# Weighted transposes with TensorE sums for the last tokens, early eviction of the fifth down product, and new PSUM bank use, in a one-core diffusion transformer layer

## The chip, the cores and the metric

The kernel runs on one core of a Trainium2 chip. The metric is device microseconds for one execution. The engines are named as in the profile: PE is TensorE's matmul, PEld its weight load, DVE VectorE, ACT ScalarE, POOL GpSimd, SP SyncE, which here issues DMAs.

## The reference

One layer over 1024 latent tokens of width 1024 with 256 context tokens, in float32: modulation by a conditioning vector, windowed and global grouped-query attention in parallel, a gated merge and an output projection, a residual LayerNorm, a feed-forward block with a depthwise convolution of width 3, and a second residual LayerNorm. Only the part from the first LayerNorm on matters here:

```python
def _conv_ffn(h, w_up, conv_w, conv_b, w_down):
    u = h @ w_up
    u = lax.conv_general_dilated(u, conv_w[:, None, :], ...) + conv_b
    gate, val = jnp.split(u, 2, axis=-1)
    return (jax.nn.silu(gate) * val) @ w_down
...
x = _layer_norm(DEEPNORM_ALPHA * x + gate1 * y, ln1_g[l], ln1_b[l])
h = x * (1.0 + scale2) + shift2
y = _conv_ffn(h, w_up[l], conv_w[l], conv_b[l], w_down[l])
x = _layer_norm(DEEPNORM_ALPHA * x + gate2 * y, ln2_g[l], ln2_b[l])
```

`w_up` has 2 x 2816 columns, `w_down` 2816 rows. `_layer_norm` subtracts the mean over the 1024 channels, scales by rsqrt(var + 1e-5), and applies a gain and a bias per channel.

## The kernel before, in words

**Products.** Activations lie with channels on the partitions and tokens along the free axis: eight channel tiles `f` of 128, two halves of 512 tokens. Every float32 product is three matmuls in a reduced type, `mm3` (L90 to L92): high x high, low x high and high x low. The high part is a ScalarE cast (L82), the low part a subtraction on VectorE or POOL (L87); both are made by `split` from raw tiles that DMAs bring.

**LN1 and the up projection.** LN1 runs in three token slices of 512, 256 and 256. For each slice `ln_steps` gives a list of steps: `stats` (TensorE column sums against a column of ones, L1028 and L1029, then tiny VectorE steps and a `pow` on POOL for the reciprocal root), `diags` (two diagonal tiles, L976), `cast` (two products with a tile of ones that spread the reciprocal root and the mean over all partitions, L1044, each copied from its PSUM bank to SBUF by ScalarE, L1046), and one `apply` for each channel tile (a multiplication L1051, a subtraction L1053, then the output). The steps wait in a list `pend`; `tick` counts TensorE's work in nanoseconds as it is written down, and lets a step into the program when its delay has gone by. For LN2 these delays are the tuples `LN2_D` (tokens 0 to 511, slice "b0") and `LN2_E` (512 to 767, "b1"): before the statistics, the diagonals, the broadcast, the first `apply`, and each further one.

The first three of 22 column blocks of the up projection are plain (`up_conv`): products on banks `u`, then the convolution `conv3` from these banks, one ScalarE pass (L1237) and two VectorE passes (L1238, L1240). The other blocks use seven products of half size with sums of weights and of the tiles `B`; those sums, `T13` and `T24`, are built by `build` (`t` on VectorE and POOL, L1075; high parts by ScalarE, L1113; low parts L1075) while the plain blocks run.

**The down projection.** It is seven products again, in the order 1, 6, 2, 7, 4, 5, 3, each over eleven inputs `k`. A product of `product(p)` fills four PSUM banks for 512 tokens, and two sets of four banks alternate (`sides`). For each input a DMA brings `rd`, ScalarE makes `hd`, VectorE `ld`. A finished product is added to the residual `zz` out of PSUM by VectorE (`accum`, L1418) in callbacks of the list `evict`, which the next product works off. LN2's slice b0 is ready when the fourth of product 4's results has been evicted, inside product 5; its steps then run by `LN2_D` in product 5: all eight multiplications on VectorE, all eight subtractions on POOL, the eight output passes `of` on ScalarE (`emit2`, L1411). Product 3 follows in two token slices of 256 with outputs `yl` (`last_mm`). Its high and low parts for inputs 0 to 6 are made long before (`D3AT`), those for 7 to 10 behind product 5's. In slice b1 the old order runs over the four `f`, inside each over inputs 0 to 6, and then again over the four `f` with inputs 7 to 10. Then the accumulations, the square sums, and the steps of LN2 by `LN2_E` follow.

**The last 256 tokens** are transposed (`tok`, L1541) so that tokens lie on partitions: two tiles of 128 tokens, each in two PSUM banks `zt`. VectorE takes the statistics from there (`bn_stats`, L1544, `bn_aggr`), POOL the `pow`, ScalarE writes `ot` = (z - mean) x rstd (L1597), and VectorE and POOL multiply by the gain and add the bias as rows `lnr` (L1586, L1588); four DMAs send the result out.

**What sets the order.** TensorE's order is the order of the program text. The other engines' queues are ordered by a scheduler from its own estimates; each engine then takes its queue strictly in turn. The functions stand below, with the line numbers of the profile.

## Time and profile before

| | us |
|---|---|
| median of 3 runs | 1600.74 (1598.96, 1600.74, 1603.09) |
| the profiled execution | 1601.19 |
| its span, first to last instruction | 1599.1 |
| TensorE busy | 1531.7 |
| VectorE, ScalarE, POOL busy | 1198.4, 813.2, 747.9 |
| mean granted TensorE clock | 0.989 |

Times of the profile count from the span's start. A row of the timeline is start, length, engine, line, operation, output<-inputs without the numbers of buffers, and in brackets how long the engine had been idle and what ended that. A matmul's length overlaps the next one's; the distance of the starts is what it costs. In the windows, each engine has its busy time and, in brackets, its instructions.

### The profile page before, as it was taken

Reading aid. Unit: us, or ns where it says so; the run is one execution under the profiler, and the core shown is the slowest. Engines: PE = TensorE matmul, PEld = TensorE weight load, DVE = VectorE, ACT = ScalarE, POOL = GpSimd, SP = SyncE. Lnnn points to the kernel's source line nnn. Section 1 sums busy time; section 2 is a strip of 40 time slices with the busy share of each in tenths; the row PEclk is TensorE's granted clock in tenths of the full one; section 3 lists DMA queues with packets and bytes.
Section 4 is the critical chain, followed back from the end, with each engine's and each line's share of the span. In section 5 each row is a group of like instructions: output and inputs, shape, how many; then the busy total and the mean of one; then the engine's idle time right before and its main releaser. Section 6 shows DMA issues by size and latency. Waiting matters only on the chain.

```text
span 1599.1 us, 22063 instructions
## 1 busy us (share of the span) xinstructions
PE 1531.7 (96%) x7680; PEld 1271.6 (80%) x7680; DVE 1198.4 (75%) x1766; ACT 813.2 (51%) x1443; POOL 747.9 (47%) x731
## 2 busy tenths in 40 slices
PE   6999999999999999999999988999999999999996
PEld 5878788888877887777688977888888888888876
DVE  7797646638888777788674887688888888657886
ACT  5422222458887566688431664454444444435542
POOL 0573302526666556565332563466767665021142
PEclk9999999999999999999999998999999999999998
DMA  9695662322237555540550222333334446996721
GB/s 377 217 317 182 217 214 80 119 81 67 58 113 161 128 138 127 124 86 18 177 179 19 93 67 92 106 106 105 106 106 109 116 119 176 375 263 209 253 100 53
DMA packets 112367, 229.98 MB, mean 144 GB/s; under 512 B 12960, under 2 KB 27808, under 8 KB 112160
## 3 DMA queue, kind: packets, MB, share of 16 engines
q1 hardware_dynamic: 96816, 198.93, 37.2%
q0 software_dynamic: 10400, 20.19, 8.2%
q10 hardware_dynamic: 5040, 9.46, 1.6%
q8 instruction: 60, 0.98, 0.3%
q14 instruction: 51, 0.42, 0.1%
HBM read 177.35 MB, written 65.86 MB: 152 GB/s over the span
## 4 chain that ended last, share of the span: by engine, by line
PE 75%; DVE 10%; ACT 4%; issue 4%; POOL 3%; DMA 3%; ACTq 0%; SPq 0%; DVEq 0%; POOLq 0%
PE ptr L531 5%; PE p L90 4%; PE p L92 4%; PE p L91 4%; PE b L92 3%; PE b L91 3%; PE b L90 3%; PE g L90 2%; PE g L92 2%; PE g L91 2%; PE av L552 2%; PE s L414 2%; PE d L91 2%; PE c L91 2%; PE a L91 2%
## 5 line engine op out<-in xcount | busy, mean ns | idle before, releaser
L541 DVE TENSOR_TENSOR ptl<-ptr,pth 128x512 fp32r<-128x512 f32 x188 | 124.7, 685 | 27.4 <-ACT pth L540 25.2
L531 PE MATMUL ptr<-ident,p 128*128 128x128 f32 x816 | 126.5, 278 | 10.4 <-DVE ptl L541 8.1
L540 ACT CAST pth<-ptr 128x512 fp32r<-128x512 f32 x188 | 106.5, 588 | 56.4 <-PE ptr L531 32.6
L87 DVE TENSOR_TENSOR ld<-rd,hd 128x1024 fp32r<-128x1024 f32 x77 | 94.0, 1240 | 53.3 <-ACT hd L82 51.0
L426 ACT ACTIVATE p<-p,nm 128x1024 f32<-128x1024 f32 (+2 forms) x128 | 125.4, 981 | 11.2 <-DVE p L459 10.5
L531 PEld LDWEIGHTS ptr<-ident,p 128*128 128x128 f32 x816 | 93.7, 140 | 40.3 <-DVE ptl L541 13.8
L82 ACT CAST hd<-rd 128x1024 fp32r<-128x1024 f32 x77 | 79.2, 1050 | 81.5 <-PE p L92 55.2
L552 PE MATMUL av<-pth,VT 128*128 128x512 f32 x236 | 104.7, 444 | 1.0 <-ACT avs L558 0.5
L90 PE MATMUL p<-hd 128*128 128x512 f32 x264 | 103.2, 391 | 0.0
L92 PE MATMUL p<-hd,ld 128*128 128x512 f32 x264 | 102.7, 389 | 0.0
L91 PE MATMUL p<-ld,hd 128*128 128x512 f32 x264 | 102.7, 389 | 0.0
L90 PE MATMUL g<-hh,whg 128*128 128x512 f32 x256 | 99.9, 390 | 0.0
L92 PE MATMUL g<-hh,wlg 128*128 128x512 f32 x256 | 99.7, 389 | 0.0
L553 PE MATMUL av<-ptl,VT 128*128 128x512 f32 x236 | 97.7, 414 | 2.0 <-POOL ptl L87 1.9
L91 PE MATMUL g<-hl,whg 128*128 128x512 f32 x256 | 99.6, 389 | 0.0
L87 POOL TENSOR_TENSOR wlg<-wg,whg 128x512 fp32r<-128x512 f32 x32 | 45.0, 1415 | 109.6 <-ACT whg L82 107.3
L459 DVE TENSOR_SCALAR_CACHE_REDUCE p<-s,cvt,nmc 128x1024 f32<-128x1024 f32 x64 | 84.5, 1340 | 12.2 <-PE s L415 12.0
L414 PE MATMUL s<-KL,q 128*128 128x512 f32 (+2 forms) x192 | 76.0, 396 | 2.9 <-ACT p_x L426 2.0
L82 ACT CAST wA<-ru 128x512 fp32r<-128x512 f32 x57 | 35.5, 623 | 76.6 <-PE d L92 34.1
L188 DVE CUSTOM_DVE_ANT_0 wml<-wml,sc,bmc 128x1024 f32<-128x1024 f32 x32 | 44.4, 1397 | 40.0 <-DMA wml<-in_wmodT_dram 37.9
L84 POOL TENSOR_SCALAR pth<-prw 128x512 fp32r<-128x512 f32 x48 | 31.1, 647 | 89.0 <-ACT prw L537 63.1
L415 PE MATMUL s<-KL,q 128*128 128x512 f32 (+2 forms) x192 | 71.6, 373 | 0.0
(396 smaller groups left out, 4989.3 us busy)
## 6 DMA issues: line engine op xcount, KB each, us to landing
wml<-in_wmodT_dram SPq DMA_DIRECT2D x48, 512.0 KB
ru<-in_w_up_dram SPq DMA_DIRECT2D x38, 512.0 KB
rd<-td SPq DMA_DIRECT2D x55, 256.0 KB
rd<-sd SPq DMA_DIRECT2D x44, 256.0 KB
rd<-in_w_dn_dram SPq DMA_DIRECT2D x33, 256.0 KB
wm<-in_wmodT_dram SPq DMA_DIRECT2D x16, 512.0 KB
wg<-in_w_g_dram SPq DMA_DIRECT2D x32, 256.0 KB
sgd<-sg ACTq DMA_DIRECT2D x32, 256.0 KB
```

Source lines behind the costliest of these rows:

```text
L82: nc.scalar.copy(hi, src)
L87: lo_eng.tensor_tensor(out=lo, in0=src, in1=hi.bitcast(F32), op=ALU.subtract)
L90: nc.tensor.matmul(ps, a[0], b[0], start=start, stop=False, skip_group_check=resumed)
L91: nc.tensor.matmul(ps, a[0], b[1], start=False, stop=False, skip_group_check=resumed)
L92: nc.tensor.matmul(ps, a[1], b[0], start=False, stop=stop, skip_group_check=resumed)
L414: nc.tensor.matmul(o, self.q[0][:, hs], ks, start=True, stop=False)
L426: nc.scalar.activation(p, s, AF.Exp, bias=nm[:, h:h + 1], scale=scale, accum_out=sm[:, h:h + 1])
L531: nc.tensor.transpose(tr[:, h * P:(h + 1) * P], self.pslice(h, n), ident)
L540: nc.scalar.copy(hi, tr)
L541: nc.vector.tensor_tensor(out=lo, in0=tr, in1=hi.bitcast(F32), op=ALU.subtract)
L552: nc.tensor.matmul(self.av, v, hi, start=first, stop=False)
L553: nc.tensor.matmul(self.av, v, lo, start=False, stop=self.left == 0)
```

## The change

- `cast` puts the two broadcast products of a slice of 256 tokens into the two halves of one PSUM bank (LN1's second and third slice, LN2's b1).
- Product 5 is added to the residual in eight `accum` calls right behind the product, ahead of the loads of product 3's last inputs, and the square sums come behind. The banks of what follows are given by hand (`pst`): slice b1's `yl` on one set of four, the transposes of channels 4 to 7 and the last slice's `yl` on the other, those of channels 0 to 3 on b1's.
- Product 3's slice b1 has the input outermost: for each of the eleven inputs all four `f`.
- For the last 256 tokens ScalarE writes the square and z x gain (`prep`); TensorE transposes the weighted tile, and sums z and its square per token by matmuls with a column of ones into a bank `st`, zeroed by a product first. The statistics come from `st`; `lnr[0]` is negated, and the end is one VectorE pass from PSUM (mean x negated gain + transposed) and one (x rstd + bias) for each of the four output tiles; one of the latter is done by ScalarE and POOL.
- The delays of LN2 are new numbers.

```diff
-LN2_D = 5000.0, 4000.0, 2500.0, 1500.0, 700.0
-LN2_E = 3500.0, 3000.0, 1500.0, 800.0, 500.0
+LN2_D = 2500.0, 500.0, 3500.0, 500.0, 700.0
+LN2_E = 5500.0, 500.0, 3500.0, 500.0, 500.0
-OTP = (0, 0), (1, 0)
+OTP = (0, 0),
...
         def cast():
+            both = sml(f"bc{nm}") if 2 * w <= HALF else None
             for i, a in enumerate("rm"):
-                ps = sml(f"bc{a}{nm}")[:, 0:w]
+                ps = sml(f"bc{a}{nm}")[:, 0:w] if both is None else both[:, i * w:(i + 1) * w]
                 nc.tensor.matmul(ps, onesf, bcs[i], start=True, stop=True)
...
-            else:
-                accum(f + 4, h1, o, False)
-                sums(f + 4, LN2_S[1], f == 0)
-
-        evict += [lambda f=f, o=acc[f]: ev(f, o) for f in range(4)]
+        if p != 5:
+            evict += [lambda f=f, o=acc[f]: ev(f, o) for f in range(4)]
         if p == 4:
             after.append(lambda: pend.extend(ln_steps(zs2, zq2, h0, "b0", emit2, *LN2_D, LN2_P[0])))
-    banks[:] = sides[nside[0] % 2] + sides[nside[0] % 2 ^ 1]
+    yb, ab = sides[nside[0] % 2], sides[nside[0] % 2 ^ 1]
+    banks[:] = [yb[3]]
+    for f in range(4):
+        accum(f + 4, h1, acc[f], False)
+        accum(f, h1, acc[f], True)
     d3 += [dload(3, k, ring) for k in range(len(D3AT), NH)]
-    for e in evict:
-        e()
+    hfree += xs
     for f in range(4):
-        accum(f, h1, acc[f], True)
+        sums(f + 4, LN2_S[1], f == 0)
 
     s = LN2_S[-1]
     w = s.stop - s.start
     nt = w // P
-    zt = {}
-    bst = post.tile([P, nt, 2, 6], F32, tag="bst", name="bst")
-    mv = post.tile([P, nt, 2], F32, tag="bmv", name="bmv")
-    nm = post.tile([P, nt], F32, tag="bnm", name="bnm")
+    def pst(n, name):
+        return ps4.tile([P, HALF], F32, tag=f"r{n}", name=name)
+    pr = [ht(f"pr{n}", (P, 4, w)) for n in range(4)]
+    nc.vector.tensor_scalar(out=pr[0][:, 3, 0:P], in0=ident, scalar1=ln2c[:, 3:4], scalar2=None, op0=ALU.mult)
+    nc.gpsimd.tensor_scalar(out=lnr[0], in0=lnr[0], scalar1=-1.0, scalar2=0.0, op0=ALU.mult, op1=ALU.add)
+    zt = {1: [pst(n, f"zt1_{n}") for n in ab[0:2]]}
+    zero4 = post.tile([P, 8], F32, tag="zero4", name="zero4")
+    nc.vector.memset(zero4, 0.0)
+    def prep(f):
+        nc.scalar.activation(pr[2 + f // 4][:, f % 4], zv(f, s), AF.Square)
+        if f != 3:
+            nc.scalar.activation(pr[f // 4][:, f % 4], zv(f, s), AF.Identity, scale=ln2c[:, f:f + 1])
 
     def tok(f):
-        if f % 4 == 0:
-            zt[f // 4] = [sml(f"zt{f}_{t}", keep=True) for t in range(nt)]
+        z, g = zv(f, s), pr[f // 4][:, f % 4]
+        if f == 4:
+            nc.tensor.matmul(st[:, 0:2 * nt], ident, zero4[:, 0:2 * nt], start=True, stop=True)
         for t in range(nt):
-            nc.tensor.transpose(zt[f // 4][t][:, (f % 4) * P:(f % 4 + 1) * P],
-                                zv(f, slice(s.start + t * P, s.start + (t + 1) * P)), ident)
-            if f % 4 == 3:
-                nc.vector.bn_stats(out=bst[:, t, f // 4], in_=zt[f // 4][t])
-
-    todo = [4, 5, 6, 7]
+            ts = slice(t * P, (t + 1) * P)
+            nc.tensor.matmul(st[:, t:t + 1], z[:, ts], onec, start=False, stop=True, skip_group_check=True)
+        for t in range(nt):
+            ts = slice(t * P, (t + 1) * P)
+            o = zt[f // 4][t][:, (f % 4) * P:(f % 4 + 1) * P]
+            if f == 3:
+                nc.tensor.matmul(o, z[:, ts], pr[0][:, 3, 0:P], start=True, stop=True)
+            else:
+                nc.tensor.transpose(o, g[:, ts], ident)
+        for t in range(nt):
+            ts = slice(t * P, (t + 1) * P)
+            nc.tensor.matmul(st[:, nt + t:nt + t + 1], pr[2 + f // 4][:, f % 4, ts], onec, start=False, stop=True,
+                             skip_group_check=True)
 
     def last_mm(o, f, r, ks):
         q = slice(r.start - HALF, r.stop - HALF)
@@ -1554,51 +1573,51 @@
             tick((r.stop - r.start) / 0.8)
 
     r = LN2_S[1]
-    yl = [sml(f"yl{f}")[:, 0:r.stop - r.start] for f in range(4)]
+    yl = [pst(n, f"yl{f}")[:, 0:w] for f, n in enumerate(yb)]
+    for k in range(NH):
+        for f in range(4):
+            last_mm(yl[f], f, r, (k,))
     for f in range(4):
-        last_mm(yl[f], f, r, range(len(D3AT)))
-    for f in range(4):
-        last_mm(yl[f], f, r, range(len(D3AT), NH))
         accum(f, r, yl[f], True)
         sums(f, r, False)
-        tok(todo.pop(0))
+    for f in range(4, KT):
+        prep(f)
+    zt[0] = [pst(n, f"zt0_{n}") for n in yb[0:2]]
+    st = pst(yb[2], "stl")
     pend += ln_steps(zs2, zq2, r, "b1", emit2, *LN2_E, LN2_P[1])
     r = LN2_S[2]
-    for f in range(4):
-        o = sml(f"yl{f}_{r.start}")[:, 0:r.stop - r.start]
+    for f, done_ in enumerate(((4, 5), (6, 7, 0), (1,), (2, 3))):
+        o = pst(ab[2 + f % 2], f"yl{f}_{r.start}")[:, 0:w]
         last_mm(o, f, r, range(NH))
         accum(f, r, o, True)
-        if todo:
-            tok(todo.pop(0))
-        todo.append(f)
+        prep(f)
+        for n in done_:
+            tok(n)
     hput(*[f"{a}d3_{k}" for k in range(len(D3AT)) for a in "hl"])
-    hfree += xs
-    tok(3)
-    for t in range(nt):
-        nc.vector.bn_aggr(out=mv[:, t], in_=bst[:, t].rearrange("p a b -> p (a b)"))
-    nc.vector.tensor_scalar(out=mv[:, :, 1], in0=mv[:, :, 1], scalar1=LN_EPS, scalar2=None, op0=ALU.add)
-    nc.gpsimd.tensor_tensor(out=mv[:, :, 1], in0=mv[:, :, 1], in1=mhalf[:, 0:nt], op=ALU.pow)
-    nc.vector.scalar_tensor_tensor(out=nm, in0=mv[:, :, 0], scalar=-1.0, in1=mv[:, :, 1], op0=ALU.mult, op1=ALU.mult)
+    sv = [post.tile([P, 2 * nt], F32, tag=f"{n}l", name=f"{n}l") for n in ("mv", "m2", "rs")]
+    mv, m2, rs = sv
+    nc.vector.tensor_scalar(out=mv, in0=st[:, 0:2 * nt], scalar1=1.0 / D, scalar2=None, op0=ALU.mult)
+    nc.vector.tensor_tensor(out=m2[:, 0:nt], in0=mv[:, 0:nt], in1=mv[:, 0:nt], op=ALU.mult)
+    nc.vector.scalar_tensor_tensor(out=rs[:, 0:nt], in0=mv[:, nt:2 * nt], scalar=LN_EPS, in1=m2[:, 0:nt],
+                                   op0=ALU.add, op1=ALU.subtract)
+    nc.gpsimd.tensor_tensor(out=rs[:, 0:nt], in0=rs[:, 0:nt], in1=mhalf[:, 0:nt], op=ALU.pow)
+    drain(OTK)
     ot = {}
-
-    def last(t, a):
+    for t, a in OTO:
+        o = ot[t, a] = ht(f"ot{t}_{a}", (P, HALF))
+        nc.vector.scalar_tensor_tensor(out=o, in0=lnr[0][:, a], scalar=mv[:, t:t + 1], in1=zt[a][t], op0=ALU.mult,
+                                       op1=ALU.add)
+    for t, a in OTO:
         o = ot[t, a]
-        nc.vector.tensor_tensor(out=o, in0=o, in1=lnr[0][:, a], op=ALU.mult)
-        e = nc.gpsimd if (t, a) in OTP else nc.vector
-        e.tensor_tensor(out=o, in0=o, in1=lnr[1][:, a], op=ALU.add)
+        if (t, a) in OTP:
+            nc.scalar.activation(o, o, AF.Identity, scale=rs[:, t:t + 1])
+            nc.gpsimd.tensor_tensor(out=o, in0=o, in1=lnr[1][:, a], op=ALU.add)
+        else:
+            nc.vector.scalar_tensor_tensor(out=o, in0=o, scalar=rs[:, t:t + 1], in1=lnr[1][:, a], op0=ALU.mult,
+                                           op1=ALU.add)
         ts = slice(s.start + t * P, s.start + (t + 1) * P)
         nc.sync.dma_start(out[4 * a:4 * a + 4, :, ts].rearrange("f p q -> p f q"),
                           o.rearrange("p (f q) -> p f q", q=P))
-
-    drain(OTK)
-    for n in OTO:
-        t, a = n
-        o = ot[n] = ht(f"ot{t}_{a}", (P, HALF))
-        nc.scalar.activation(o, zt[a][t], AF.Identity, bias=nm[:, t:t + 1], scale=mv[:, t, 1:2])
-        drain(max(len(pend) - OTA, 0))
-    for t, a in OTO:
-        last(t, a)
-        drain(max(len(pend) - OTB, 0))
     drain()
     order.close()
     ps4.release()
```

The instructions move on the engines as follows. ScalarE in product 5, before: `hd_7` to `hd_10` are the high parts of product 5's last four inputs, `rbb` and `mbb` the copies of LN2's two broadcasts, `of` the output passes of b0.

```order
L82 CAST hd_7_14592<-rd_7_14589 128x1024
L82 CAST hd_8_14611<-rd_8_14608 128x1024
L82 CAST hd_9_14634<-rd_9_14631 128x1024
L82 CAST hd_10_14661<-rd_10_14658 128x1024
L1046 COPY rbb_14646<-bcrb_14644 128x512
L1046 COPY mbb_14650<-bcmb_14648 128x512
L1411 ACTIVATE of_0_14670<-zz_0_13226,ln2c 128x512
L1411 ACTIVATE of_0_14678<-zz_0_13228,ln2c 128x512
```

The same place now, from the copies on:

```order
L1045 COPY rbb_14609<-bcrb_14607 128x512
L1045 COPY mbb_14613<-bcmb_14611 128x512
L80 CAST hd_9_14665<-rd_9_14662 128x1024
L1410 ACTIVATE of_0_14617<-zz_0_13224,ln2c 128x512
L1410 ACTIVATE of_0_14635<-zz_0_13226,ln2c 128x512
L1410 ACTIVATE of_0_14643<-zz_0_13228,ln2c 128x512
L1410 ACTIVATE of_0_14651<-zz_0_13230,ln2c 128x512
L1410 ACTIVATE of_0_14659<-zz_0_13224,ln2c 128x512
L1410 ACTIVATE of_0_14674<-zz_0_13226,ln2c 128x512
L1410 ACTIVATE of_0_14682<-zz_0_13228,ln2c 128x512
L1410 ACTIVATE of_0_14690<-zz_0_13230,ln2c 128x512
L80 CAST hd_10_14699<-rd_10_14696 128x1024
```

The four high parts stood ahead of the copies; now `hd_9` stands behind them, and `hd_10` behind all eight output passes.

ScalarE where the third plain block of the up projection begins, before: `c_0_10220` and `c_0_10224` are the first two convolution passes from the banks `u`, `hwu` high parts of weights, `T13h` and `T24h` those of the sums of `B`.

```order
L1113 CAST T13h_10427<-t_2_10397 128x1024
L1237 ACTIVATE c_0_10220<-u_0_9854,cvt 128x1024
L82 CAST hwu_2_10313<-rwu_2_10311 128x1024
L82 CAST hwu_2_10386<-rwu_2_10384 128x1024
L1237 ACTIVATE c_0_10224<-u_0_9855,cvt 128x1024
L1113 CAST T24h_10440<-t_2_10412 128x1024
L1113 CAST T13h_10469<-t_3_10463 128x1024
```

And now:

```order
L1112 CAST T13h_10425<-t_2_10395 128x1024
L1112 CAST T24h_10438<-t_2_10410 128x1024
L1112 CAST T13h_10467<-t_3_10461 128x1024
L1112 CAST T24h_10471<-t_3_10464 128x1024
L80 CAST hwu_2_10311<-rwu_2_10309 128x1024
L1236 ACTIVATE c_0_10218<-u_0_9854,cvt 128x1024
L80 CAST hwu_2_10384<-rwu_2_10382 128x1024
L1236 ACTIVATE c_0_10222<-u_0_9855,cvt 128x1024
```

The first convolution pass, which stood behind one `T13h`, has three more casts of sums and one of weights ahead of it.

VectorE at the same place, before: `t` are sums of `B`, `T13l` and `T24l` low parts, `c_0` the convolution's two passes (L1238, L1240) from bank `u`.

```order
L1075 TENSOR_TENSOR t_2_10412<-z_0_9071,t_2_10412 128x512
L1075 TENSOR_TENSOR T13l_10428<-t_2_10397,T13h_10427 128x1024
L1238 SCALAR_TENSOR_TENSOR c_0_10220<-u_0_9854,cvt,c_0_10220 128x1023
L1075 TENSOR_TENSOR t_3_10466<-v_9972,t_3_10463 128x512
L1240 SCALAR_TENSOR_TENSOR c_0_10220<-u_0_9854,cvt,c_0_10220 128x1023
L1238 SCALAR_TENSOR_TENSOR c_0_10224<-u_0_9855,cvt,c_0_10224 128x1023
L87 TENSOR_TENSOR lwu_2_10314<-rwu_2_10311,hwu_2_10313 128x1024
```

And now:

```order
L1074 TENSOR_TENSOR T13l_10426<-t_2_10395,T13h_10425 128x1024
L1074 TENSOR_TENSOR t_3_10464<-v_9971,t_3_10461 128x512
L1074 TENSOR_TENSOR T24l_10439<-t_2_10410,T24h_10438 128x1024
L1074 TENSOR_TENSOR T13l_10468<-t_3_10461,T13h_10467 128x1024
L1074 TENSOR_TENSOR T24l_10472<-t_3_10464,T24h_10471 128x1024
L1237 SCALAR_TENSOR_TENSOR c_0_10218<-u_0_9854,cvt,c_0_10218 128x1023
L1239 SCALAR_TENSOR_TENSOR c_0_10218<-u_0_9854,cvt,c_0_10218 128x1023
L1237 SCALAR_TENSOR_TENSOR c_0_10222<-u_0_9855,cvt,c_0_10222 128x1023
```

Low parts that stood behind the convolution's passes now stand ahead of them.

More of the change, by code (lines that the diff above doesn't have):

```diff
@@ L51 @@
 RAWB = 3
-OTP = (0, 0), (1, 0)
+OTP = (0, 0),
 OTO = (0, 0), (0, 1), (1, 0), (1, 1)
 OTK = 4
-OTA = 1
-OTB = 2
 PSU = 6, 7, 2, 3, 4, 5, 0, 1
@@ L1430, in layer_kernel, with sml @@
     banks = list(PSO)
-    def sml(name, w=512, keep=False):
+    def sml(name, w=512):
         n = banks.pop(0)
-        if not keep:
-            banks.append(n)
+        banks.append(n)
         return ps4.tile([P, w], F32, tag=f"r{n}", name=name)
@@ L1589, in last @@
+    for t, a in OTO:
+        o = ot[t, a]
+        if (t, a) in OTP:
+            nc.scalar.activation(o, o, AF.Identity, scale=rs[:, t:t + 1])
+            nc.gpsimd.tensor_tensor(out=o, in0=o, in1=lnr[1][:, a], op=ALU.add)
+        else:
+            nc.vector.scalar_tensor_tensor(out=o, in0=o, scalar=rs[:, t:t + 1], in1=lnr[1][:, a], op0=ALU.mult,
+                                           op1=ALU.add)
         ts = slice(s.start + t * P, s.start + (t + 1) * P)
```

1 line of the change is left out of this document (removed).

## Prediction, made before the run

> **What bounds the kernel now.** I read first the page's busy times and its chain of work that ended last.
>
> ```profile
> PE 1531.7 (96%) x7680; PEld 1271.6 (80%) x7680; DVE 1198.4 (75%) x1766; ACT 813.2 (51%) x1443; POOL 747.9 (47%) x731
> PE 75%; DVE 10%; ACT 4%; issue 4%; POOL 3%; DMA 3%; ACTq 0%; SPq 0%; DVEq 0%; POOLq 0%
> ```
>
> TensorE is busy 96% of the span. Then its waits around LN1 (total, times, longest):
>
> ```profile
> PE u L90 <- ACT T24h L1113: 6.7, 1, 6.7
> ```
>
> And the windows from there on: TensorE's busy time is the first figure behind the length, the granted clock the third from a row's end.
>
> ```profile
> 960.00:970.00 10.00, 6.42 (x16) 5.07 (x17) 10.00 (x10) 9.37 (x10) 1.88 (x2) 0.52 0.24 73
> 980.00:1540.00 560.00, 560.00 (x2477) 463.38 (x2476) 435.44 (x406) 265.03 (x343) 268.70 (x163) 1.00 0.53 160
> 1550.00:1560.00 10.00, 6.23 (x51) 5.84 (x51) 9.83 (x15) 4.55 (x8) 0.00 (x0) 1.00 0.08 28
> 1560.00:1570.00 10.00, 10.00 (x73) 10.00 (x73) 7.60 (x17) 1.68 (x4) 0.00 (x0) 0.83 0.00 0
> ```
>
> From 980 to 1540 us TensorE is busy 560.00 of 560 us at a clock of 1.00, so what delays it ahead of 980 us is not made good later, and a hole made inside that stretch adds in full. What a change can win lies in three places: the gap of 6.7 us ahead of 963.6 us, the hole in 1550–1560 us with the low clock after it, and the end.
>
> The profiled execution took 1601.19 us with a span of 1599.1, so 2.1 us lie around the span; it stands 0.45 above the median of 1600.74. I sum in span time and add the sum to the median. About 0.3%, 4.8 us, is what a measurement of this kernel can tell from no change.
>
> **Part A, the shared bank of the two broadcast products.** `cast` now puts both products of a 256-token slice into one PSUM bank, and ScalarE copies the first out before the second is written. The rows of LN1's last slice, a bank each, from the timeline (start, length, engine, line, operation, in brackets the idle time before it and what ended that), as all rows below:
>
> ```profile
> 928.67 1.19 PE L1044 MATMUL bcra<-dgra,onesf 128*128 128x256 f32 x2 [2.36 <-DVE dgra L976]
> 929.66 1.06 PE L1044 MATMUL bcma<-dgma,onesf 128*128 128x256 f32 x2
> 932.16 0.35 ACT L1046 COPY rba<-bcra 128x256 f32<-128x256 f32 x1
> ```
>
> The copy ran at 932.16, queued behind `affine` passes of the slice before. If the second product must wait for it, it goes from 929.66 to 932.16 + 0.35 + 0.1 = 932.6: 2.9 us later, with the whole rest of the product on `u` queued behind it on TensorE. The trace has no two products in one bank, so the bounds are 0 (disjoint columns need no wait) and 2.9; I take 2.9, since the copy's place is a row. [...] It costs nothing in the end: TensorE's work on `u` ends 2.9 later and then meets the 6.7 us gap of part B. Were that gap gone, 2.9 would be its price.
>
> **Part B, the gap at 957–964 us.** TensorE stops because the next product writes bank `u` of the third plain block, which its convolution still reads.
>
> ```profile
> 963.58 0.76 PE L90 MATMUL u<-B,hwu 128*128 128x512 f32 x1 [6.68 <-ACT T24h L1113]
> 957.47 1.04 ACT L1113 CAST T13h<-t 128x1024 fp32r<-128x1024 f32 x1 [6.62 <-DVE t L1075]
> 958.42 1.20 ACT L1237 ACTIVATE c<-u,cvt 128x1024 f32<-128x1024 f32 x1
> 959.52 1.98 ACT L82 CAST hwu<-rwu 128x1024 fp32r<-128x1024 f32 x2
> 962.50 1.04 ACT L1113 CAST T24h<-t 128x1024 fp32r<-128x1024 f32 x1
> 959.22 1.22 DVE L1075 TENSOR_TENSOR T13l<-t,T13h 128x1024 fp32r<-128x1024 f32 x1
> 960.36 1.28 DVE L1238 SCALAR_TENSOR_TENSOR c<-u,cvt,c 128x1023 f32<-128x1023 f32 x1
> 961.55 0.68 DVE L1075 TENSOR_TENSOR t<-v,t 128x512 f32<-128x512 f32 x1
> 962.15 1.28 DVE L1240 SCALAR_TENSOR_TENSOR c<-u,cvt,c 128x1023 f32<-128x1023 f32 x1
> 962.38 1.28 POOL L1075 TENSOR_TENSOR t<-z,t 128x512 f32<-128x512 f32 x1 [5.55 <-DVE t L1075]
> ```
>
> The view names T24h, whose end (963.54) fits; the second convolution pass on VectorE ended at 963.43, and fits as well. I choose the convolution, since the stopped product reads `B` and `hwu` and writes `u`, and T24h is none of these. In the changed order ScalarE has T24h, T13h and T24h (three casts more) and one hwu ahead of the first convolution pass, and VectorE three low parts ahead of its first. Along ScalarE: T13h ends 958.5; T24h and T13h, at 1.04 each, are over by 961.4 at the latest; the last T24h waits for VectorE's `t` (after T13l, 960.4–961.0) and POOL's `t` behind it (1.28, to 962.4), so it ends 963.4; hwu to 964.4; the convolution pass to 965.6. VectorE's two passes then take 1.28 + 1.28 less an overlap of 0.1: 968.1, and TensorE starts at 968.2 in place of 963.58: **+4.6**. The low end, +3.5, has POOL's pass at VectorE's pace; the high end, +6.3, has LN1's last subtractions late by part A's wait.
>
> **Part C, the fifth product.** LN2's first slice of 512 tokens fires its statistics 2.7 us sooner and its broadcast seven triples of matmuls sooner. More important is ScalarE's queue: its cast of the fifth product's last input (`hd_10`) now stands behind all eight output passes `of`, which wait one by one for POOL.
>
> ```profile
> 1521.40 0.39 PE L90 MATMUL p<-hd 128*128 128x512 f32 x1
> 1524.12 0.28 PE L1028 MATMUL stb<-onec,zs 128*128 128x1 f32 x2
> 1525.82 0.49 PE L90 MATMUL p<-hd 128*128 128x512 f32 x1
> 1532.77 1.02 PE L1044 MATMUL bcrb<-dgrb,onesf 128*128 128x512 f32 x2
> 1544.06 0.28 PE L90 MATMUL yl<-hd 128*128 128x256 f32 x1
> 1520.15 2.58 DVE L996 TENSOR_TENSOR zq<-zq,sqb 128x512 f32<-128x512 f32 x2
> 1532.69 1.23 DVE L87 TENSOR_TENSOR ld<-rd,hd 128x1024 fp32r<-128x1024 f32 x1 [1.30 <-ACT hd L82]
> 1534.45 11.50 DVE L1051 TENSOR_TENSOR zz<-zz,rbb 128x512 f32<-128x512 f32 x8 [0.53 <-ACT rbb L1046]
> 1535.35 13.00 POOL L1053 TENSOR_TENSOR zz<-zz,mbb 128x512 f32<-128x512 f32 x8 [7.64 <-ACT mbb L1046]
> 1531.60 1.05 ACT L82 CAST hd<-rd 128x1024 fp32r<-128x1024 f32 x1 [1.66 <-PE p L92]
> 1548.39 0.81 ACT L1411 ACTIVATE of<-zz,ln2c 128x512 f32<-128x512 f32 x1 [0.44 <-POOL zz L1053]
> ```
>
> All in the times of before. One input of the product is twelve matmuls: 1524.12 − 1521.40 = 2.72. The statistics now stand at 1521.40, but the squares are summed only at 1520.15 + 2.58 = 1522.73: after the column sums that can go, TensorE waits 1.1. The broadcast stands one input and nine matmuls on: 1522.8 + 1.7 (1525.82 − 1524.12) + 2.72 + 2.04 = 1529.3. POOL begins 1535.35 − 1532.77 = 2.58 later, at 1531.9, and needs 13.0, or 14.2 if the low part of input 9 (1.23), which now stands among VectorE's multiplications, holds it up: 1544.9 to 1546.1. The last `of` ends 0.85 behind, `hd_10` takes 1.05 and its low part 1.23: 1548.0 to 1549.2. TensorE reaches that input at 1544.06 − 2.72 + 1.1 = 1542.4 and needs the low part at its second matmul, 0.2 later: it stands still 5.4 to 6.6 us. Afterwards it is slow for a while, as after the hole of before: 10 us at a clock of 0.83 are 1.7 lost. Together 1.1 + 5.4..6.6 + 1.7: 8.2 to 9.4, and 10.5 if the slow stretch is as deep as in 960–970 us (0.52). I take **+8.8**. Were POOL at the 1.28 of its lone pass above (10.2 for eight), the standstill would still be 2.6.
>
> [...] In the rows a multiplication beside POOL takes 11.50 / 8 = 1.44 and a subtraction 1.63, less than a multiplication at 0.68 and a lone subtraction at 1.28 one behind the other (1.96). [...] The trace's 13.0 decides.
>
> The evictions of the fifth product, eight in a row on VectorE ahead of two low parts, take 8 × 0.68:
>
> ```profile
> 1558.37 2.72 DVE L1418 SCALAR_TENSOR_TENSOR zz<-p,nmod,zz 128x512 f32<-128x512 f32 x4
> ```
>
> That is 5.4 us, hidden under the input-outermost product 3 that needs those low parts only nine inputs on, 9 × 12 matmuls of 0.12, 13 us after it starts: nothing. If product 3 caught up, the wait would be the difference.
>
> **Part D, product 3 in its two slices,** from 1544.06 to the last matmul's end at 1584.45, 40.4 us.
>
> ```profile
> 1559.17 0.33 PE L1541 MATMUL zt<-ident,zz 128*128 128x128 f32 x1 [3.44 <-DVE zz L1418]
> 1570.41 0.28 PE L1028 MATMUL stb<-onec,zs 128*128 128x1 f32 x2
> 1571.22 0.36 PE L90 MATMUL yl<-hd 128*128 128x256 f32 x1
> 1575.26 0.38 PE L1541 MATMUL zt<-ident,zz 128*128 128x128 f32 x2
> ```
>
> The hole of 3.44 + 0.3 goes, for the accumulations are done early and the transposes stand behind a finished `prep`; so does its slow stretch, 1.7. What is late next is nothing of VectorE's in the first slice. In come 24 one-column sums: four cost 1571.22 − 1570.41 = 0.81, so 24 cost 4.9, and I take 5.2 since each now stands between other instructions; two transposes fewer in the stretch save 0.2, and one broadcast waits for its copy, 0.6. −5.4 + 5.2 − 0.2 + 0.6: **+0.2**, between −0.6 and +1.
>
> **Part E, the end,** now 1599.1 − 1584.45 = 14.6 us.
>
> ```profile
> 1584.65 0.48 DVE L1418 SCALAR_TENSOR_TENSOR zz<-yl,nmod,zz 128x256 f32<-128x256 f32 x1 [1.32 <-PE yl L92]
> 1585.56 1.30 DVE L1544 BATCH_NORM_STATS2 bst<-zt 128x6 f32<-128x512 f32 x2 [0.42 <-PE zt L1541]
> 1588.44 2.78 ACT L1597 ACTIVATE ot<-zt,bnm,bmv 128x512 f32<-128x512 f32 x4 [3.39 <-DVE bnm L1581]
> 1594.58 0.69 DVE L1588 TENSOR_TENSOR ot<-ot,lnr 128x512 f32<-128x512 f32 x1
> ```
>
> Behind the last accumulation (1585.1) there come now the square on ScalarE, the last sums and transposes (to 1586.5), three tiny VectorE steps (0.5), four passes from PSUM and three from SBUF at 0.68 each, seven for 4.8, with the `pow` on POOL under the first four: 1591.8 to 1592.6 in place of 1595.27. The 3.8 us from there to the span's end are output DMAs and stay, up to 0.6 longer for queueing. **−2.5**, between −1.7 and −3.4.
>
> **Sum.** 0 + 4.6 + 8.8 + 0.2 − 2.5 = +11.1: from 1600.74 to 1611.8, about 1612. The ends of the parts give 1608 to 1617.
>
> **Rivals.** (1) T24h really is what released TensorE. For it: the view says so, and its end is 0.04 before the start. Against: the product doesn't read it. T24h then ends 2.1 to 3.2 us sooner, B is −3.2, the sum +3.3: 1604. Chance 0.06. (2) Not slower: ScalarE's `hd_10` is no bottleneck, because POOL's subtractions, begun sooner and with fewer low parts beside them, finish before TensorE needs the input. It decides at 1542.6 − 1.23 − 1.05 − 0.85 = 1539.5, a POOL train of 7.6 us, 0.95 a pass where even the lone one took 1.28. C is then at most 1.1, less if the statistics' wait goes too, and the sum 2.3 to 3.4: 1603. Chance 0.10. (3) Neither queue matters, only D and E: 1598.4. Chance 0.05. (4) C comes and B does not: +6.5, 1607; chance 0.05. (5) By mutual exclusion on VectorE and POOL or two slow stretches: over 1617, chance 0.08. The forecast, both standstills, has 0.66.
>
> **Numbers.** Below 1602.5 lie half of rival 2 and rival 3, 0.10; above 1617 lies 0.08: the range is 1602.5 to 1617. Slower by over 0.3% (1605.5): the forecast, 4, 5 and a part of 2, 0.82; within: rival 1, most of 2 and 3, 0.15; faster: the far end of 3 with part E larger than priced, 0.03.
>
> **What would show it.** In the profile of the changed kernel TensorE's gap before the third plain block's successor should be about 8.4 us long (6.7 + 4.6, less the 2.9 of part A) and end with VectorE's second convolution pass; there should be a new standstill of 5 to 7 us at the last of the fifth product's eleven inputs, ended by a low part, with its `hd` cast behind the eighth `of`; no hole in product 3's first slice; and 12 us from the last matmul of product 3 to the end. I am wrong if TensorE stays busy through the fifth product, or if the first gap ends with T24h while the convolution still runs.

## The result, and the profile after

The changed kernel takes 1616.55 us (median of 6 runs, 1612.62 to 1619.38) against 1601.24 for the kernel before in the same runs: ratio 1.0094, 95% interval 1.0078 to 1.0109. It is 15 us slower. The profiled execution took 1619.38 with a span of 1617.3; it is the longest of the six, so the profiles below differ by a little more than the medians.

TensorE's waits from LN1 on in the changed kernel that the prediction speaks of (total, times, longest). Before, the long ones were the 6.7 us at `u` and 4.1 us at `zt`, in product 3:

```profile
PE u L88 <- DVE c L1239: 8.3, 1, 8.3
PE p L88 <- ACT hd L80: 5.0, 1, 5.0
PE bca L1043 <- ACT rba L1045: 3.5, 2, 3.1
PE stb L1027 <- DVE zq L994: 1.0, 1, 1.0
PE p L89 <- DVE ld L85: 0.5, 1, 0.5
PE bcb L1043 <- ACT rbb L1045: 0.5, 1, 0.5
```

Every wait that the prediction named stands here with the cause that it named: the convolution's second VectorE pass (L1239) at the gap, the late high part `hd` and then its low part `ld` in product 5, the copy `rba` at LN1's shared bank, the squares `zq` at the early statistics, the copy `rbb` at the shared bank of LN2's slice b1. TensorE also waits for a diagonal tile, `dgra`, 2.4 us before and 1.4 now. The hole of 3.4 us in product 3 is gone.

The rows at the end of the gap:

```profile
964.20 1.04 ACT L1112 CAST T24h<-t 128x1024 fp32r<-128x1024 f32 x1 [2.00 <-POOL t L1074]
968.65 1.28 DVE L1239 SCALAR_TENSOR_TENSOR c<-u,cvt,c 128x1023 f32<-128x1023 f32 x1
970.08 0.77 PE L88 MATMUL u<-B,hwu 128*128 128x512 f32 x1 [8.28 <-DVE c L1239]
```

The convolution's pass ends at 969.93, just ahead of TensorE's restart; the cast T24h had ended at 965.24, 4.8 us earlier.

The windows of the same stretches, columns as before (the last is the end of the span):

```profile
960.00:970.00 10.00, 1.80 (x16) 1.59 (x14) 9.11 (x9) 7.64 (x8) 2.11 (x1) 0.78 0.00 0
970.00:980.00 10.00, 9.92 (x32) 7.95 (x33) 9.96 (x9) 5.02 (x5) 4.07 (x3) 0.71 0.42 154
980.00:1540.00 560.00, 558.79 (x2463) 461.88 (x2462) 432.10 (x403) 263.46 (x342) 268.14 (x163) 1.00 0.52 160
1550.00:1560.00 10.00, 4.54 (x12) 3.00 (x11) 7.05 (x7) 6.21 (x7) 4.23 (x3) 0.80 0.28 106
1590.00:1617.00 27.00, 16.71 (x128) 16.17 (x127) 13.32 (x26) 7.56 (x16) 5.50 (x6) 0.82 0.26 78
```

The emptiest windows are where the gap and product 5's last input lie now; the long middle is as full as before. The clock of 0.82 in the last row is in part that of the end, where TensorE runs out of work (before, 0.78 in 1573–1599 us), but a part lies in 1590–1600 us, where TensorE is busy at a clock of 0.83; nothing in the prediction accounts for that, and it returns below.

Where the 18.2 us between the two spans lie, worked out from the starts of rows: LN1's first column sum, TensorE's restart at the third plain block, product 3's first matmul, its last one, and the span's end.

| stretch | before | changed | difference | forecast |
|---|---|---|---|---|
| start to LN1's first sum | 869.99 | 871.55 | +1.6 | 0 |
| to the restart (parts A, B) | 93.59 | 98.53 | +4.9 | +4.6 |
| to product 3 (part C) | 580.48 | 592.10 | +11.6 | +8.8 |
| product 3 (part D) | 40.27 | 42.41 | +2.1 | +0.2 |
| the end (part E) | 14.77 | 12.71 | −2.1 | −2.5 |

The first row is code that the change doesn't touch; between profiles of all the kernels here it lies anywhere from 867.6 to 873.9. Below, profiles are therefore compared from LN1's first sum on ("from LN1": 729.1 before, 745.7 changed), and times by ratio to the kernel before on the same chip.

ScalarE, POOL and TensorE in product 5 of the changed kernel, rows of the timeline that answer to the `hd`, `of` and `mbb` rows of before:

```profile
1540.19 1.06 ACT L80 CAST hd<-rd 128x1024 fp32r<-128x1024 f32 x1
1541.74 0.82 ACT L1410 ACTIVATE of<-zz,ln2c 128x512 f32<-128x512 f32 x1 [0.49 <-POOL zz L1052]
...
1554.26 0.81 ACT L1410 ACTIVATE of<-zz,ln2c 128x512 f32<-128x512 f32 x1 [0.41 <-POOL zz L1052]
1554.98 3.87 ACT L80 CAST hd<-rd 128x1024 fp32r<-128x1024 f32 x4
1540.16 8.88 POOL L1052 TENSOR_TENSOR zz<-zz,mbb 128x512 f32<-128x512 f32 x5 [6.86 <-ACT mbb L1045]
1549.67 4.56 POOL L1052 TENSOR_TENSOR zz<-zz,mbb 128x512 f32<-128x512 f32 x3 [0.63 <-DVE zz L1050]
1528.16 0.38 PE L1026 MATMUL stb<-onec,zs 128*128 128x1 f32 x2 [0.25 <-POOL zs L993]
1529.50 0.38 PE L1027 MATMUL stb<-onec,zq 128*128 128x1 f32 x2 [0.96 <-DVE zq L994]
...
1556.06 0.79 PE L88 MATMUL p<-hd 128*128 128x512 f32 x1 [5.00 <-ACT hd L80]
1557.32 0.79 PE L89 MATMUL p<-ld,hd 128*128 128x512 f32 x1 [0.47 <-DVE ld L85]
```

Eight output passes, each behind its subtraction on POOL (1540.16 to 1554.23), with ScalarE idle for 0.41 to 1.48 us ahead of each, and four casts behind the eighth; TensorE goes on when the first of the four is done, and at about half its pace: from 1557.91 on a matmul of 512 columns comes every 0.43 us, where before the standstill one came every 0.227.

And the last VectorE pass of the end, which answers to the one that ended at 1595.27:

```profile
1610.29 2.86 DVE L1616 SCALAR_TENSOR_TENSOR ot<-ot,rsl,lnr 128x512 f32<-128x512 f32 x3
```

It ends at 1613.15, and the output DMAs take the remaining 4.1 us.

### The profile page after: what moved, and what is told of

The parts are those of the page before. It is cut to its first block, busy times and chain, and to the rows that moved or that the text cites. A ratio compares the mean times of both kernels' runs of the same rounds, so it can differ in the third digit from the quotient of the medians.

```text
span 1617.3 us, 22206 instructions
## 1 busy us (share of the span) xinstructions
PE 1546.3 (96%) x7748; PEld 1283.3 (79%) x7748; DVE 1200.8 (74%) x1764; ACT 816.4 (50%) x1455; POOL 746.5 (46%) x731
## 4 chain that ended last, share of the span: by engine, by line
PE 77%; DVE 11%; ACT 4%; DMA 3%; issue 3%; POOL 2%; SPq 0%; DVEq 0%; ACTq 0%; POOLq 0%
PE ptr L529 5%; PE g L88 3%; PE g L90 3%; PE g L89 3%; PE b L90 3%; PE b L89 3%; PE b L88 3%; PE s L412 2%; PE av L550 2%; PE d L89 2%; PE c L89 2%; PE a L89 2%; PE c L90 2%; PE a L90 2%; PE d L90 2%
```

## The experiments

All ratios are to the kernel before. "Lost" is the sum of what matmuls took beyond their usual pitch (0.227 us for 512 columns, 0.12 for 256). A "slow stretch" is a run of matmuls at about half that pace (0.43 and 0.21 us in the changed kernel).

| run | ratio | 95% interval | from LN1, us |
|---|---|---|---|
| changed kernel | 1.0094 | 1.0078–1.0109 | 745.7 |
| 1 before, shared banks only | 1.0034 | 1.0021–1.0047 | 736.4 |
| 2 changed, LN1's banks apart | 1.0067 | 1.0046–1.0089 | 740.2 |
| 3 changed, convolution first | 1.0066 | 1.0041–1.0091 | 736.2 |
| 4 changed, old delays in LN2's b0 | 1.0018 | 1.0005–1.0031 | 732.0 |
| 5 changed, both undone | 0.9988 | 0.9979–0.9997 | 728.1 |
| 6 changed, last high part on VectorE | 1.0080 | 1.0066–1.0093 | 744.4 |
| 7 changed, statistics late again | 1.0086 | 1.0069–1.0103 | 742.5 |
| 8 changed, transposes spread | 1.0096 | 1.0083–1.0109 | 742.5 |
| 9 as 5, spread, casts behind the convolution | 0.9981 | 0.9970–0.9992 | 725.3 |
| 10 as 5, spread, sums behind the convolution | 0.9937 | 0.9926–0.9949 | 718.1 |
| 11 before, sums behind the convolution | 0.9946 | 0.9932–0.9959 | 721.3 |
| 12 as 10, shared banks back | 0.9926 | 0.9912–0.9939 | 720.7 |

The intervals of runs 2, 3, 6, 7 and 8 overlap that of the changed kernel: what they show is read from their profiles, one execution each. Behind LN1's first eight column sums, which no run edits, the profiles of runs 2, 5, 6 and 8 have a slow stretch of some 1.6 us and the others none; it is contained in their last column.

**1. The shared bank by itself.** The kernel before, with this edit alone:

```diff
         def cast():
+            both = sml(f"bc{nm}") if 2 * w <= HALF else None
             for i, a in enumerate("rm"):
-                ps = sml(f"bc{a}{nm}")[:, 0:w]
+                ps = sml(f"bc{a}{nm}")[:, 0:w] if both is None else both[:, i * w:(i + 1) * w]
```

> The kernel before with one edit: the two broadcast products of a 256-token slice share a PSUM bank. Theory (the queue order at the convolution is the price): 4 to 6 us slower than before, with TensorE's gap ahead of the third plain block ended by the convolution's second VectorE pass and some 8 us long after a wait of 3 us at the shared bank. Rival (the shared bank is hidden by the gap and the change's loss lies elsewhere): within 1 us of before. Second rival (the bank waits themselves are the price, not the queues): 3 us slower, gap as long as before.

TensorE's rows with a wait in it, around LN1:

```profile
930.83 1.22 PE L1045 MATMUL bca<-dgma,onesf 128*128 128x256 f32 x2 [3.07 <-ACT rba L1047]
967.59 0.77 PE L90 MATMUL u<-B,hwu 128*128 128x512 f32 x1 [8.52 <-DVE c L1241]
```

The bank's wait is 3.07, the gap 8.52, and from LN1's first sum to the restart it takes 98.53 us, as in the changed kernel to the hundredth. So this edit in a LayerNorm step is all of part B. From LN1 on the profile is 7.3 us longer than before, of which 4.9 lie there and 1.7 in product 3 (41.99 us against 40.27), where the hole of before has a longer slow stretch behind it.

**2. The shared bank taken out of the changed kernel,** for LN1's slices alone (`... if 2 * w <= HALF and nm[0] == "b" else None`).

> The changed kernel with LN1's broadcasts in banks of their own again (LN2's slice of 256 tokens keeps the shared bank). Theory: 5 us faster than the changed kernel, so 10 us slower than before, with the gap at the convolution at 6.7 us again and product 5 as slow as in the changed kernel. Rival (the two stretches interact through the clock or the DMAs): a gain under 3 us.

The gap is 6.72 us again and product 5's standstill stays at 4.99. The ratio falls by 0.0027, less than the two intervals resolve; from LN1 it is 5.5 us less. The times do show this price elsewhere: 5.4 us in run 1, and 0.0030 of the ratio, 4.8 us, from run 4 to run 5, whose intervals lie apart.

**3. The wait or the order?** The shared bank does two things: it makes TensorE wait 3.07 us, and with it the scheduler puts casts and low parts ahead of the convolution (presumably because it reckons `u` to come later; no run shows its reckoning). Here the wait stays and the order is forced back by a data dependence that adds zero:

```diff
+    gz = []
+
+    def gate(t):
+        nc.vector.tensor_tensor(out=t[:, 0, 0:1], in0=t[:, 0, 0:1], in1=gz[0], op=ALU.add)
+
     def build(k):
...
+            if (k, a) in ((2, "24"), (3, "13"), (3, "24")):
+                gate(st[a])
             nc.scalar.copy(tp[a + "h", k], st[a])
             sub(e, tp[a + "l", k], st[a], tp[a + "h", k].bitcast(F32))
...
             conv3(t, ups.pop((j, gv))[0], gv * NF + j)
+            if not gz:
+                gz.append(post.tile([P, 1], F32, tag="gz", name="gz"))
+                nc.vector.tensor_scalar(out=gz[0], in0=t[:, 0:1], scalar1=0.0, scalar2=None, op0=ALU.mult)
```

> The changed kernel, shared banks and their waits kept, but three casts of sums are made to depend on the first convolution (a zero taken from its output is added to one column of them), so that ScalarE and VectorE take the convolution first. Theory (the order of the two queues is the price, the bank's wait costs nothing): the 3 us wait at the bank stays, the gap at the convolution ends 5 to 6 us sooner, and the kernel is 5 to 6 us faster than the changed one. Rival (the bank wait itself is the price): no gain over 1 us.

TensorE's waits around LN1 in this run:

```profile
PE bca L1043 <- ACT rba L1045: 3.5, 2, 3.1
PE u L88 <- DVE c L1246: 2.8, 1, 2.8
PE bca L1043 <- DVE dgra L974: 1.4, 1, 1.4
```

The 3.1 us at the bank are still there, the gap has gone from 8.3 to 2.8, and LN1's first sum to the restart takes 93.0 us, 5.5 less than in the changed kernel and 0.6 less than before. So the order of the queues was the price, and the bank's wait was covered. Another 3.7 us go from the restart to product 3, 1.6 of them since this profile has no slow stretch behind the statistics; its execution (1607.69) is the shortest of the run's four, 3.5 below their median, and in the times the gain of 0.0028 isn't resolved.

**4. The delays.** The changed kernel with `LN2_D = 5000.0, 4000.0, 2500.0, 1500.0, 700.0`.

> The changed kernel with the old delays for LN2's first slice (5000, 4000, 2500, 1500, 700). ScalarE's four high parts of product 5 then stand ahead of the broadcast copies again. Theory (hd_10 behind eight output passes, and the early statistics, are product 5's price): TensorE's 5 us standstill and the two slow stretches in product 5 go, the kernel is 10 to 12 us faster than the changed one, so 4 to 6 us slower than before. Rival (the eight evictions ahead of the low parts cost as much): a gain under 6 us and a new hole in product 3.

The view lists no wait of TensorE in product 5 any more: from the restart to product 3 it takes 580.2 us, where the changed kernel takes 592.1 and before 580.5. The gain is 12 us by ratio, at the expectation's edge. The evictions ahead of the low parts make no hole.

**5. Both undone** (the edits of 2 and 4).

> The changed kernel with LN1's broadcasts in banks of their own and with the old delays for LN2's first slice: only the weighted transposes, the sums on TensorE, the early evictions, product 3's order and the bank plan are left of the change. Theory (the two losses are independent and add): the changed kernel less 5 and less 11 to 12, so 0 to 2 us faster than before; from LN1's first column sum to the span's end 727 us, where before has 729.1. Rival (with both gone something else is late): 3 us or more slower than before.

What is left of the change gains 1 us from LN1 on and 2 us by ratio: the end is 2.1 us shorter (12.69 against 14.77), product 3 is 0.3 longer (40.60 against 40.27), the stretch from the restart to product 3 is 0.8 shorter (579.68 against 580.48), and a slow stretch behind LN1's first sums, which that profile shows and the one of before doesn't, costs it 1.6.

**6. ScalarE's queue by itself.** In `dload`, `split(r, h, l, nc.vector if (p, k) == (5, NH - 1) else nc.scalar, nc.vector)`.

> The changed kernel with the high part of product 5's last input cast on VectorE instead of ScalarE, all delays kept. Theory (ScalarE's queue of eight output passes is what holds that input): TensorE's 5 us standstill shrinks to 1 to 3 us, since VectorE is free for the cast at its last multiplication, some 3 us ahead of ScalarE's; 2 to 4 us faster than the changed kernel. [...]

```profile
PE p L88 <- DVE hd L84: 2.5, 1, 2.5
PE p L89 <- DVE ld L85: 1.7, 1, 1.7
PE stb L1027 <- DVE zq L994: 1.0, 1, 1.0
```

The standstill is 4.3 us (2.55 + 1.71 by the rows), not 1 to 3: VectorE comes to the cast only behind its eight multiplications, which run beside POOL's train to 1549.13, and then takes 1.75 us for the cast and 2.17 for its low part, where a low part took 1.23 by itself. Time gained from the restart to product 3: 2.6 us, inside the 2 to 4 expected, but only 1.2 of it is standstill, and 1.0 a shorter slow stretch behind it. So ScalarE's queue did hold the input, but VectorE's, behind its multiplications, holds it nearly as long.

**7. The statistics by themselves:** `LN2_D = 5000.0, 500.0, 1000.0, 500.0, 700.0`, so the broadcast stays early.

> The changed kernel with LN2's first delays 5000, 500, 1000 in place of 2500, 500, 3500: the statistics stand where they stood before, the broadcast stays early. Theory: the wait of 1 us for the squares goes, and the slow stretch behind it with it, so product 5 is 1 to 3 us shorter; the standstill at its last input stays at 5 us, since the output passes still stand ahead of its cast. Rival (the early statistics set the standstill too): it falls under 3 us.

The wait for `zq` and the slow stretch behind the statistics are gone, the 5.02 us standstill is not. From the restart to product 3: 589.1 us, 3.0 less than the changed kernel. By ratio the gain doesn't stand out from the intervals.

**8. The transposes spread,** `((4, 5), (6, 7), (0, 1), (2, 3))` in the last loop.

> The changed kernel with the transposes and sums of the last tokens spread over the four last products as two, two, two, two instead of two, three, one, two; the rest kept. Theory (three such groups in a row, 3.1 us of matmuls of one or 128 columns, let the clock be lowered for one stretch): no slow stretch in product 3's last slice, 1.6 us faster than the changed kernel from LN1 on. Rival (the slow stretch is set by when product 5's standstill ended, not by the groups): a slow stretch of 1 to 1.6 us in product 3 still.

The changed kernel's windows here, with a clock of 0.83 in the second row:

```profile
1580.00:1590.00 10.00, 10.00 (x90) 10.00 (x89) 3.25 (x13) 1.46 (x4) 0.70 (x1) 1.00 0.01 2
1590.00:1600.00 10.00, 9.54 (x67) 9.09 (x67) 2.60 (x7) 1.56 (x4) 0.73 (x1) 0.83 0.00 0
```

And with the groups spread:

```profile
1580.00:1590.00 10.00, 10.00 (x91) 10.00 (x90) 2.19 (x8) 1.63 (x4) 0.70 (x1) 1.00 0.01 2
1590.00:1600.00 10.00, 9.54 (x79) 9.09 (x78) 6.21 (x13) 4.64 (x11) 3.08 (x4) 1.00 0.16 54
```

In this profile the slow stretch is gone, and product 3 takes 40.60 in place of 42.41. The runs' median doesn't follow (1.0096 against 1.0094): whatever the spreading gives isn't seen in the time. Runs 4 and 5 keep the three groups in a row and show no slow stretch either, so three in a row don't suffice for one.

**9 to 12. A better version.** Run 3 had shown that the convolution can be put first; before's own gap of 6.7 us has the same cause. Run 9 has runs 2, 4 and 8 and four casts behind the convolution.

> The kernel of the two undone losses, and besides: four casts of sums made to wait for the first convolution, as in the run with the added zero, and the transposes of the last tokens spread over the products as two, two, two, two instead of two, three, one, two. Theory (each standstill removed adds in full): the gap at the convolution is 1 us shorter than before's, no slow stretch behind the transposes, 2 to 5 us faster than before. Rival (what is gained at the convolution is late at the products with the sums): within 1 us of the kernel with the two losses undone.

The gap is 5.7 us: VectorE still makes five sums ahead of the convolution's passes. Run 10 holds the sums themselves back, in place of the casts:

```diff
+    gz = []
...
         def s1():
             st["13"] = t = tm(f"t13_{k}").rearrange("p (a q) -> p a q", a=2)
+            if k > 1:
+                nc.vector.tensor_tensor(out=b12[:, 0:1], in0=b12[:, 0:1], in1=gz[0], op=ALU.add)
             sub(nc.vector, t[:, 1], b12, b11)
...
             cv.append(t)
+            if not gz:
+                gz.append(post.tile([P, 1], F32, tag="gz", name="gz"))
+                nc.vector.tensor_scalar(out=gz[0], in0=t[:, 0:1], scalar1=0.0, scalar2=None, op0=ALU.mult)
```

> As the run that put the casts of sums behind the first convolution and spread the transposes, but the sums of the last two channel groups themselves wait for the first convolution (a zero taken from its output is added to one column of an input). Theory (TensorE's gap ahead of the third plain block is set by VectorE reaching the convolution's two passes, and the sums are not needed for another 30 us): the gap shrinks from 5.7 to 1 to 3 us, 3 to 4 us faster than that run, 5 to 8 us faster than before. Rival (the sums are then late for the products that use them): what the gap gives comes back as a wait at the first product with sums.

VectorE in this run at the place of the old gap:

```profile
952.56 1.21 DVE L1074 TENSOR_TENSOR T24l<-t,T24h 128x1024 fp32r<-128x1024 f32 x1
953.70 1.27 DVE L1241 SCALAR_TENSOR_TENSOR c<-u,cvt,c 128x1023 f32<-128x1023 f32 x1
955.00 1.28 DVE L1243 SCALAR_TENSOR_TENSOR c<-u,cvt,c 128x1023 f32<-128x1023 f32 x1
...
965.77 0.68 DVE L1074 TENSOR_TENSOR t<-v,z 128x512 f32<-128x512 f32 x1
```

And its windows:

```profile
950.00:980.00 30.00, 29.93 (x158) 25.72 (x157) 29.93 (x30) 15.21 (x16) 10.49 (x6) 1.00 0.26 88
980.00:1530.00 550.00, 550.00 (x2432) 454.84 (x2431) 434.96 (x404) 265.71 (x345) 271.84 (x166) 1.00 0.53 162
```

The convolution's second pass ends at 956.28, when TensorE is just coming to the bank, and TensorE's idle time there is under 0.1 us; its clock stays at 1.00, and the sums, 10 us later, are in time. That is more than expected: 10 us faster than before by ratio, since both the gap of 6.7 and the 2.6 us lost at half pace behind it go.

Run 11 is the kernel before with that one edit.

> The kernel before with one edit: the sums of the last two channel groups wait for the first convolution. Theory (the gap of 6.7 us and the slow stretch behind it are all that the edit takes, whatever the rest of the change): no gap ahead of the third plain block, 8 to 10 us faster than before, product 5 and the end as before. Rival (the gain of the last run came from the change's parts together): under 5 us.

It is 8.7 us faster than before by ratio, with a gap of 0.4: nearly all of run 10's gain has nothing to do with the change.

Run 12 is run 10 with LN1's shared banks back, where the prediction put a price of 2.9 on the bank's wait if the gap were gone.

> The fastest kernel so far (sums behind the first convolution) with the shared bank of LN1's two broadcasts put back. Theory (with the gap gone, the wait at the shared bank has no cover, as the prediction priced it): TensorE waits 3.1 us at the second product, the wait is not made good, and the kernel is 2 to 4 us slower than that one. Rival (the convolution has slack that takes it up): less than 1 us slower.

```profile
PE bca L1043 <- ACT rba L1045: 3.5, 2, 3.1
PE bca L1043 <- DVE dgra L974: 1.4, 1, 1.4
```

The profile has the wait, no gap to cover it, and 720.7 us from LN1 where run 10 has 718.1: 2.6 more, as priced. The times don't confirm it: 0.9926 lies at the edge of run 10's interval, on the other side, and run 12's profiled execution (1593.11) is the longest of its five, 2.3 above their median. With the runs at hand the price of that wait stays open between 0 and 2.6 us.

## Why the prediction was right

It forecast 1612, slower, and the time is 1616.55, near the upper end of its range of 1602.5 to 1617. The two queues that it named were the price; that the time stayed inside the range is in part luck, since two of the five parts, C and D, ended above their own high ends, and what rival 5 had over 1617, two slow stretches, is what came.

- **Part A, right.** The second product waited 3.07 for the copy. It went 2.1 us later than before, counted from LN1's first sum, not 2.9, since the first one went 0.65 sooner; but a longer slow stretch behind it (2.2 us lost, before 1.1) brought TensorE to the gap 3.3 later. That cost nothing at the end, by run 3. The two products write disjoint columns of the bank, and in the changed kernel and runs 1, 3, 6, 7, 8 and 12 the second waited 3.1 us for the copy all the same; with a bank each, before and in runs 9, 10 and 11, it had no wait. So the value 0 that I kept as the other bound is out.
- **Part B, right.** +4.9 for +4.6, ended by L1239, with a gap of 8.28 where some 8.4 were forecast. The choice against the view's T24h (rival 1) is settled by the changed kernel's own rows, where T24h ended 4.8 us ahead of the restart, and by runs 3, 9 and 10: with the convolution ahead of the casts or sums the gap shrinks or goes. Run 2's profile again names T24h for a gap of 6.72 that, with the order of before, the convolution ends.
- **Part C, right in mechanism, mis-sized.** The term was 8.8 and measured 11.6. The statistics' wait was 0.25 + 0.96 = 1.2 (1.1), the standstill 5.00 + 0.47 = 5.5 (5.4 to 6.6), POOL's eight subtractions 14.1 us from first to last (13.0 to 14.2), each as the first fence on product 5 shows it; the input waited first for its high part, then for the low part that the forecast named. The step that failed is "Afterwards it is slow for a while", with its 1.7 lost: two slow stretches came, 1.6 lost behind the statistics and 2.9 from the standstill on (twelve matmuls in 6.12 us with 0.47 of waiting, where they take 2.72). The part's own high end, 10.5 for a clock of 0.52, was too low as well: reckoned like the 1.7 (10 us times 0.17), that clock would have given 4.8 lost, near the 4.5 that came. The first stretch went with the statistics' wait in run 7, but runs 2, 3 and 8 kept a wait of 0.5 to 0.7 and only run 2 shows it, so what sets it is open. Rival 2, the input in time, is out by the standstill itself.
- **Part D, wrong in size.** +2.1 for +0.2, above its own high end of +1. The 24 sums and 12 transposes cost what the rows said (one channel tile: 0.45 + 0.25 + 0.36 = 1.06 us), and where no slow stretch falls into it, in runs 4, 5, 8, 9 and 10, product 3 takes 40.6, +0.3. The broadcast's wait for its copy was 0.46 (0.6). The remainder is the slow stretch of run 8's first fence, 1.6 lost, and the end of part C's. Here too a slow stretch is what I left out; what sets it is open, as said below.
- **Part E, right.** −2.1 for −2.5; the last VectorE pass ended 8.4 us behind product 3's last matmul, where before took 10.8: 2.4 gained, a little under the 2.7 to 3.5 reckoned, since the three passes from SBUF took 2.86 in place of 3 times 0.68. The output DMAs took 4.1 in place of 3.8.
- **The sum.** +11.1 forecast against +16.6 from LN1 in the profiles and +15.3 in the medians. Of the 5.5 us between the first two, 4.4 lie in slow stretches that the sum didn't have (2.8 in part C, 1.6 in part D); the rest is 0.3 to 0.4 each in parts B, D and E.

That VectorE and POOL exclude each other, as rival 5 has it, no run shows. Eight pairs one behind the other would take 8 × (0.68 + 1.28) = 15.7 us, an estimate from the passes of before; the changed kernel took 14.1 for the eight pairs and a low part beside them, where the rows of before gave 14.2.

## What to carry to other kernels

An edit's price may lie far from the edit. Sharing a bank cost nothing where it made TensorE wait, since a gap lay behind, and 5 us where the scheduler's new order let other work pass ahead of the one pass that frees a bank; so compare the queues of every engine around the bottleneck's next wait, not only the lines that were edited. A queue in which a short step feeds the bottleneck and long trains wait on a third engine is worth a look for what stands behind the train. And a gap that is already there can be read the same way: asking which pass frees the bank, and what stands ahead of it, was worth 9 us in a kernel whose TensorE was busy 96% of its span.

## What the runs showed of the hardware

- TensorE's pace fell to about half behind a stretch that the profile counts as busy. In the changed kernel, after three groups of one-column sums and transposes (1589.47 to 1592.58, no idle), matmuls of 256 columns come every 0.21 us in place of 0.12:

```profile
1592.21 0.50 PE L1564 MATMUL stl<-onec,pr 128*128 128x1 f32 x4
1592.58 0.36 PE L88 MATMUL yl<-hd 128*128 128x256 f32 x1
...
1593.37 0.28 PE L88 MATMUL yl<-hd 128*128 128x256 f32 x1
1593.49 0.34 PE L89 MATMUL yl<-ld,hd 128*128 128x256 f32 x1
1593.63 0.42 PE L90 MATMUL yl<-hd,ld 128*128 128x256 f32 x1
...
1596.62 0.41 PE L89 MATMUL yl<-ld,hd 128*128 128x256 f32 x1
1596.83 0.36 PE L90 MATMUL yl<-hd,ld 128*128 128x256 f32 x1
```

  The stretch lasts from 1593.49 to 1596.83, 3.3 us, and begins 0.9 us after the small matmuls ended. The same three groups have a slow stretch behind them in some profiles (the changed kernel, runs 2, 3, 6 and 7: 1.4 to 1.6 us lost) and none in others (runs 4 and 5), and LN1's first column sums, the same code in all, have one behind them in four profiles (some 1.6 us) and none in the others. Runs 4 and 5 keep the three groups in a row but also lack product 5's standstill, so what sets the slow stretch stays open.
- The releaser that the view of waits names for a bank can be an instruction that only ends at about the same time: for the gap of before it names a cast that the stopped matmul doesn't read (T24h ended at 963.54, the convolution's second pass at 963.43, and the matmul started at 963.58).
